# The low half of every second weight chunk of six output panels, made by an adding DMA instead of VectorE

## The chip, the cores and the metric

The program runs on one NeuronCore of one Trainium2 chip, in one launch. The metric is the device time of one execution in microseconds (us), taken as the median of three executions. Beside it stands one profiled execution, from which every duration below comes.

## The reference

The layer takes 256 tokens of width 4096 and 256 memory tokens. One input projection makes the columns of three head groups and their gates, the groups are computed, gated and concatenated, and one output projection with a residual and a layer norm ends it. Everything is float32.

```
proj = x @ w_in                      # (256 x 4096) @ (4096 x 11280)
c_a, c_b, c_gate, g_q, g_k, g_v, g_lr, g_gate, m_q, m_gate = split(proj)
y_conv = conv_group(c_a, c_b, ...) * silu(c_gate)
y_gla  = gla_group(g_q, g_k, g_v, g_lr, ...) * silu(g_gate)
y_mem  = memory_group(m_q, mem @ w_mem_kv) * silu(m_gate)
mixed  = concatenate([y_conv, y_gla, y_mem])
out    = mixed @ w_out               # (256 x 4096) @ (4096 x 4096)
x      = layernorm(2**0.25 * x + out) * ln_g + ln_b
```

## The kernel before

[...] ScalarE rounds `raw` to `hi` (line 89) and VectorE subtracts to get `lo` = `raw` - `hi` (line 90). A product is then three passes: hi by hi, hi by the activation's low half, and lo by hi.

All weight matrices are cut into panels of up to 512 columns, and a panel into 16 chunks of two blocks of 128 rows each. A chunk is a tile of 128 partitions by 1024 float32, 512 KB. The function `panel` runs over the chunks of one panel: it loads a chunk from memory on SyncE's DMA queue (line 115), splits it, and issues 12 matmuls (line 279), for two token tiles of 128: eight that read `hi` and, behind them, four that read `lo`. The work comes in this order: memory keys and values (lines 146 to 180), 23 panels of the input projection with the three head groups' own work woven in, and 8 panels of the output projection (lines 934 to 952, here n = 0 to 7).

The tiles that carry the chunks come from pools: six buffers for `raw`, four for `hi` and four for `lo`. So ScalarE can round a chunk only when TensorE is done with the `hi` of four chunks before, and a load can start only when an earlier `raw` has been read for the last time. Every engine works through its own queue in order. The order within the queues is made by a scheduler when the program is built, and semaphores tie the queues together.

At the end of an output panel VectorE adds the panel's two banks to the residual (line 929) and takes its statistics (line 932), and GpSimd multiplies the panel by a row of the norm's gain (line 946), which a small DMA has spread over the partitions (line 924). The last panel, n = 7, holds its last six chunks in other buffers and ends one token tile before the other, so that the final norm can overlap.

Of the kernel before, what the change touches and what calls it, by code (L numbers as in the profile page):

```python
# [9 lines left out]
F32 = mybir.dt.float32  # L10
F32R = mybir.dt.float32r
BF16 = mybir.dt.bfloat16
AF = mybir.ActivationFunctionType
ALU = mybir.AluOpType
# [3 lines left out]
P = 128  # L18
D = 4096
KT = D // P  # L20
# [9 lines left out]

C_A, C_B, C_G, G_Q, G_K, G_V, G_LR, G_G, M_Q, M_G = 0, 1024, 2048, 3072, 4096, 5120, 7168, 7184, 9232, 10256

# (name, index, column ranges of w_in)
PANELS = (
    [("cb", 0, [(C_B, 512)]), ("ca", 0, [(C_A, 512)])]
    + [("cb", 1, [(C_B + 512, 512)]), ("ca", 1, [(C_A + 512, 512)])]
# [12 lines left out]
def layer_kernel(ctx, tc, xT, memT, xres, w_mem, w_in, w_out, cst, w_gate,  # L49
                 conv_g, conv_b, norm_g, ln_g, ln_b, out):  # L50
    nc = tc.nc
# [8 lines left out]
    acc = ctx.enter_context(tc.tile_pool(name="acc", bufs=4, space=PSUM))  # L60
    sm = ctx.enter_context(tc.tile_pool(name="sm", bufs=4, space=PSUM))

    # SBUF in units of 4 KB a partition, each handed out again once it is given back
    free_units = deque(range(NUNITS))
    unit_of = {}
    serial = [0]
# [18 lines left out]
        return small.tile([P, n], F32, tag=f"little{n}", name=f"{name}_{serial[0]}")  # L85

    def halves(src, hi, lo):
        """fp32 as hi + lo, each exact in the 12 bits the PE multiplies."""
        nc.scalar.copy(out=hi, in_=src)  # L89
        nc.vector.tensor_tensor(out=lo, in0=src, in1=hi.bitcast(F32), op=ALU.subtract)  # L90

# [17 lines left out]
            unit([P, 4, 256], F32R, f"l{name}"),  # L109
        )  # L110

    def load(tiles, ap, a=None, b=None):
        """DRAM -> raw -> hi + lo, of columns or k-tiles a to b."""
        raw, hi, lo = (t[:, a:b] for t in tiles)
        nc.sync.dma_start(out=raw, in_=ap[:, a:b])  # L115
        halves(raw, hi, lo)
        return tiles[1], tiles[2]

    work = deque()
    fill = deque()  # L120

    def do_work(n):
        """Up to n pieces of queued work; None ends the turn."""
        for _ in range(min(n, len(work))):
            f = work.popleft()
            if f is None:
                break
            f()
# [1 line left out]
    def pause(n=1):  # L130
        work.extend([None] * n)

# [1 line left out]
    def four(ap):  # L134
        return ap.rearrange("p (k t) -> p k t", k=4)

# [2 lines left out]
    mem_banks = [acc.tile([P, 512], F32, tag="acc", name=f"mk_{i}") for i in range(4)] + [  # L139
        bank("mv") for _ in range(4)  # L140
    ]
    # the array's clock comes up while the first loads are under way
    idle = nc.const_aps.tensor(1.0, [P, 512], BF16)
    for _ in range(WARM):
        nc.tensor.matmul(mem_banks[7], lhsT=idle[:, 0:P], rhs=idle, start=True, stop=True)
# [53 lines left out]
        for mt in range(2):  # L199
            halves(mem_banks[4 + nb * 2 + mt], mvh[nb][:, mt, :], mvl[nb][:, mt, :])  # L200

    # A transpose without the PE: DVE transposes the 32 x 32 blocks in their places, copies between
    # groups of 32 partitions put the blocks where they belong
    def queue_transpose(src, dst, then, back=False):
        """Token-major [P, 2, 512] -> feature-major [P, 4, 256], or back. dst() is asked for the
        tile when the first block moves; then(tile) is queued behind the last."""
        st = {}

        def blocks():
            t = tmp.tile([P, 1024], F32, tag="T", name=f"T_{serial[0]}", bufs=1)  # L210
            serial[0] += 1
            nc.vector.transpose(out=t, in_=src.rearrange("p a b -> p (a b)"))  # L212
            give(src)
            st["t"] = t

        def moves(b):
            if b == 0:
                st["d"] = dst()
            tok = "p t (q j c) -> p t q j c"
            feat = "p q (t i c) -> p t q i c"  # L220
            flat = "p (q t i c) -> p t q i c" if back else "p (t q j c) -> p t q j c"
            sizes = dict(q=4, t=2, c=32)
            frm = st["t"].rearrange(flat, **sizes)
            to = st["d"].rearrange(tok if back else feat, c=32, **({"q": 4} if back else {"t": 2}))
            for a in range(4):
                f = nc.scalar.copy if a % 2 else nc.vector.tensor_copy
                f(  # L227
                    out=to[32 * b : 32 * b + 32, :, :, a, :],
                    in_=frm[32 * a : 32 * a + 32, :, :, b, :],
                )  # L230

        work.append(blocks)
        for b in range(4):
            work.append(lambda b=b: moves(b))
        work.append(lambda: then(st["d"]))

    def queue_halves(src, then):
        """Token-major [P, 2, 512] -> feature-major hi and lo, for then(hi, lo)."""

        def scratch():  # L240
            serial[0] += 1
            return tmp.tile([P, 4, 256], F32, tag="S", name=f"S_{serial[0]}", bufs=1)

        def go(d):
            hi, lo = unit([P, 4, 256], F32R, "xh"), unit([P, 4, 256], F32R, "xl")
            halves(d, hi, lo)
            then(hi, lo)

        queue_transpose(src, scratch, go)
# [3 lines left out]
        queue_halves(mk[i], lambda hi, lo, i=i: mkT.update({i: (hi, lo)}))  # L253

    def products(ps, terms):
        """Sum over (stationary hi, lo), (moving hi, lo) pairs of three exact passes each."""
        n = len(terms)
        for t, ((sh, sl), (mh, ml)) in enumerate(terms):
            for k, (a, b) in enumerate(((sh, mh), (sl, mh), (sh, ml))):
                nc.tensor.matmul(  # L260
                    ps, lhsT=a, rhs=b, start=t == 0 and k == 0, stop=t == n - 1 and k == 2
                )

# [1 line left out]
    def panel(chunks, width, stat, fills=0, apart=0, soon=KT // 2):  # L265
        """stat(kt // 4) gives the stationary hi and lo. The products of the last `apart` chunks
        are left to the caller, as a function of the chunk's place and the token tile."""
        banks = []
        for tt in range(2):
            serial[0] += 1  # L270
# [15 lines left out]

        for c in range(KT // 2):
            tiles = w_tiles([P, 2, width], "w", KT // 2 - apart <= c < KT // 2 - WBUFS)
            hi, lo = load(tiles, chunks[c].rearrange("p (k n) -> p k n", k=2))
            if c >= KT // 2 - apart:  # L290
                held.append((c, hi, lo))
            else:
                for w in (hi, lo):
                    for tt in range(2):
                        mms(c, tt, w, w is lo)
            left = max(1, soon - c)
            do_work(-(-len(work) // left))
            for _ in range(min(fills, len(fill))):
                fill.popleft()()
# [10 lines left out]
    mixT = {}  # L310

    def queue_mix(src, key):
        """Token-major mixed columns -> feature-major hi and lo."""
        queue_halves(src, lambda hi, lo: mixT.update({key: (hi, lo)}))

# [1 line left out]
    mo = {}  # L317

    def queue_memory(i, mq):
# [73 lines left out]
        pause(2)  # L393
        work.append(probs)

# [1 line left out]
    qT, kT, v, o = {}, {}, {}, {}  # L397
    gate = {}

    def queue_lr(lr):  # L400
        def weights():
            # rows 0-15 and 32-47 hi, rows 64-79 lo, against hi, lo and hi of lr
            raw = unit([P, 1024], F32, "wgraw")
            w = unit([P, 1024], F32R, "wg")
            nc.gpsimd.memset(raw, 0.0)
            for r in (0, 32, 64):
                nc.sync.dma_start(out=raw[r : r + 16, :], in_=w_gate)
            nc.scalar.copy(out=w, in_=raw)
            nc.vector.tensor_tensor(
                out=w[64:96, :], in0=raw[64:96, :], in1=w[64:96, :].bitcast(F32), op=ALU.subtract  # L410
            )
            give(raw)
            gate["w"] = w
# [16 lines left out]
        pause(2)  # L430

    def queue_gates(i):
        """Decays of heads 2*i, 2*i+1, applied to queries and keys."""
        st = {}

        def logits(pair):
# [71 lines left out]
            give(kT[i])  # L508

        def composites():  # L510
            # ca: [end-decayed 0 | 1] for chunk 1, [end-decayed 0, through chunk 1 | end-decayed 1]
            # for chunks 2 and 3; cb: [end-decayed 2 | 3] for chunk 3, queries [2 | 3 through chunk 2]
            kt_, ks, el, q = gate[i][0], st["cs"], st["el"], qT[i]
            ca = unit([P, 4, 256], F32, "ca")
            cb = unit([P, 4, 256], F32, "cb")
# [27 lines left out]
    def queue_head(h):  # L543
# [3 lines left out]
        def attn():  # L547
# [21 lines left out]
            for nm in ("Ah", "Al"):  # L569
                st["a"].append(tmp.tile([P, 512], F32R, tag=nm, name=f"{nm}_{h}", bufs=1))  # L570
            halves(ps[:, :384], *(t[:, :384] for t in st["a"]))
            # keys s of a tile against tokens c of the same tile: keep c >= s
            for t in st["a"]:
                diag = t.rearrange("p (t c) -> p t c", t=2)[:, :, 0:P]
                nc.gpsimd.affine_select(
# [41 lines left out]
        work.append(lambda: outputs(0))  # L617
        work.append(lambda: outputs(1))

# [1 line left out]
    conv = {"h": {}, "y": {}}  # L621

    def queue_conv(i):
# [85 lines left out]
            for tt in range(2):  # L709
                work.append(lambda i=i, tt=tt: norm(i, tt))  # L710

# [1 line left out]
    sig = {}  # L713
    off = 0
    for name, i, ranges in PANELS:
# [93 lines left out]
        give(hi, lo)  # L809
    assert not fill  # L810

# [1 line left out]
    keys = [("gla", i) for i in range(4)] + [("conv", i) for i in range(2)] + [  # L813
        ("mem", i) for i in range(2)
    ]

    # y = (z g) rstd - mu rstd g + b: z g as z comes, the rest a product of -mu rstd and 1
    # with g and b, g hi in rows 0 and 32, lo in 64, b hi in row 1, lo in 65
    gb = []

    def rows_gb(j):
# [16 lines left out]
    def stat(u):  # L838
        return mixT[keys[u]]

    z = []
# [92 lines left out]
    for n in range(8):  # L934
# [3 lines left out]
        nc.sync.dma_start(out=xr, in_=xres[n].rearrange("p (t d) -> p t d", t=2))  # L938
        z.append(xr)
        if n < 7:  # L940
            banks = panel(w_out[n], 512, stat, soon=KT // 2 if n else 10)
            g = spread(ln_g, n, "S")
            for tt in range(2):
                residual(tt, n, banks[tt])
                y = z[n][:, tt, :]
                nc.gpsimd.tensor_tensor(out=y, in0=y, in1=g, op=ALU.mult)

    # the last panel ends with the first token tile, so that its norm runs beside the second's
    banks, rest = panel(w_out[7], 512, stat, apart=APART)
    g, beta = spread(ln_g, 7, "S"), spread(ln_b, 7, "Ah")  # L950
    for k in range(APART):
# [104 lines left out]
```

## Time and profile before

| what | value |
|---|---|
| three executions | 1541.36, 1542.34, 1542.21 us; median 1542.21 us |
| profiled execution, first to last instruction | 1539.6 us |
| difference between that span and the median | 2.6 us (1542.21 - 1539.6) |
| TensorE's granted clock, mean of the span | 0.997 |
| ScalarE and GpSimd, busy | 740.7 us (48%) and 68.0 us (4%) |
| moved by DMA | 307.56 MB, mean 200 GB/s |
| all DMA issues | on SyncE's queue; none on GpSimd's |

The time of the profiled execution is known by its span alone, from its first to its last instruction; the 2.6 us around it are launch and end, as far as the two numbers can be compared. The share of busy time of an engine is an average over the whole span. What a stage is worth is read from that stage: which engine has no gap there, and which wait ends last. The busy time of matmuls overlaps, since each starts before the one ahead has left the array, so their rate is read from a chain of many.

### The profile page before, as it was taken

What the parts mean: (1) busy time and instruction counts of PE and PEld (TensorE: products, weight loads), DVE (VectorE), ACT (ScalarE), POOL (GpSimd) and SP (SyncE); (2) the same over time, 40 slices, a digit from 0 to 9 for tenths busy, and PEclk for the clock granted to TensorE, in tenths of its full rate; (3) what the DMA queues carried; (4) which work ended last, traced back from release to release, by engine and by line L of the source; (5) the groups of instructions that cost most, each with busy time, mean ns of one, the idle gap of its engine ahead of it and who ended that gap; (6) DMA issues with size and microseconds to landing.
All of it is one profiled execution on the core that took longest, in us unless ns stands there. A gap on an engine that the chain in (4) does not pass through costs nothing.

```text
span 1539.6 us, 18667 instructions
## 1 busy us (share of the span) xinstructions
PE 1526.9 (99%) x6977; PEld 1292.9 (84%) x6977; DVE 980.6 (64%) x1227; ACT 740.7 (48%) x898; POOL 68.0 (4%) x71
## 2 busy tenths in 40 slices
PE   9999999999999999999999999999999999999997
PEld 7888888888888888999998888888888888888885
DVE  6555654999999555857575555555557555455555
ACT  6444653444566344655454554455556333333341
POOL 0000000000000000003030000000000000000001
PEclk9999999999999999999999999999999999999998
DMA  8777676666656666565555566666677666666662
GB/s 326 245 251 249 190 210 193 190 197 188 193 163 178 218 192 188 161 191 175 167 170 195 179 195 205 193 193 195 195 233 253 216 196 196 206 202 199 198 199 109
DMA packets 89363, 307.56 MB, mean 200 GB/s; under 512 B 9972, under 2 KB 10868, under 8 KB 89272
## 3 DMA queue, kind: packets, MB, share of 16 engines
q1 hardware_dynamic: 89272, 306.38, 63.0%
q8 instruction: 54, 0.88, 0.2%
q14 instruction: 37, 0.30, 0.1%
HBM read 302.14 MB, written 4.19 MB: 199 GB/s over the span
## 4 chain that ended last, share of the span: by engine, by line
PE 98%; DVE 1%; DMA 0%; issue 0%; SPq 0%; ACT 0%; POOL 0%; DVEq 0%; ACTq 0%
PE acc L279 85%; PE mk L169 5%; PE mv L169 5%; PE o L260 1%; PE A L561 1%; PE sc L260 0%; PE mo L260 0%; DMA rawwm<-w_mem 0%; DVE xr L915 0%; SPq L115 0%; PE mg L905 0%; DVE nz L502 0%; POOL xr L913 0%; DVE cc L870 0%; DVE low L90 0%
## 5 line engine op out<-in xcount | busy, mean ns | idle before, releaser
L90 DVE TENSOR_TENSOR low<-raww,hiw 128x1024 fp32r<-128x1024 f32 (+2 forms) x496 | 603.5, 1219 | 427.5 <-ACT hiw L89 422.3
L89 ACT CAST hiw<-raww 128x1024 fp32r<-128x1024 f32 (+2 forms) x496 | 507.6, 1027 | 640.7 <-PE acc L279 612.4
L279 PE MATMUL acc<-hiw,hx 128*128 128x512 f32 (+2 forms) x1472 | 560.3, 381 | 0.0
L279 PE MATMUL acc<-hiw,lx 128*128 128x512 f32 (+2 forms) x1472 | 560.3, 381 | 0.0
L279 PE MATMUL acc<-low,hx 128*128 128x512 f32 (+2 forms) x1472 | 381.6, 380 | 0.0
L279 PEld LDWEIGHTS acc<-hiw,hx 128*128 128x128 f32 x1472 | 276.4, 188 | 45.4
L279 PEld LDWEIGHTS acc<-hiw,lx 128*128 128x128 f32 x1472 | 276.3, 188 | 45.2
L279 PEld LDWEIGHTS acc<-low,hx 128*128 128x128 f32 x1472 | 275.3, 188 | 45.4
L279 PE MATMUL acc<-hiw,xh 128*128 128x512 f32 x512 | 199.3, 389 | 0.0
L279 PE MATMUL acc<-hiw,xl 128*128 128x512 f32 x512 | 199.2, 389 | 0.0
L279 PE MATMUL acc<-low,xh 128*128 128x512 f32 x512 | 137.8, 389 | 0.0
L279 PEld LDWEIGHTS acc<-hiw,xl 128*128 128x128 f32 x512 | 96.1, 188 | 20.0
L279 PEld LDWEIGHTS acc<-low,xh 128*128 128x128 f32 x512 | 96.1, 188 | 19.9
L279 PEld LDWEIGHTS acc<-hiw,xh 128*128 128x128 f32 x512 | 96.1, 188 | 19.9
L90 DVE TENSOR_TENSOR lowm<-rawwm,hiwm 128x1024 fp32r<-128x1024 f32 (+2 forms) x68 | 78.3, 1160 | 53.2 <-ACT hiwm L89 52.6
L649 DVE SCALAR_TENSOR_TENSOR cacc<-hT,cst_sb,cacc 128x231 f32<-128x231 f32 (+29 forms) x240 | 98.0, 462 | 0.1
L89 ACT CAST hiwm<-rawwm 128x1024 fp32r<-128x1024 f32 (+2 forms) x68 | 67.6, 1002 | 62.8 <-PE mv L169 30.9
L169 PE MATMUL mk<-hiwm,hmem 128*128 128x512 f32 (+1 forms) x132 | 50.7, 387 | 0.4 <-ACT hiwm L89 0.4
L169 PE MATMUL mk<-hiwm,lmem 128*128 128x512 f32 (+1 forms) x132 | 50.4, 384 | 0.0
L227 ACT COPY S<-T 32x256 f32<-32x256 f32 x112 | 45.2, 404 | 9.9 <-DVE T L212 8.5
L169 PE MATMUL mv<-hiwm,hmem 128*128 128x512 f32 x128 | 49.9, 390 | 0.0
L169 PE MATMUL mv<-hiwm,lmem 128*128 128x512 f32 x128 | 49.8, 389 | 0.0
(179 smaller groups left out, 752.5 us busy)
## 6 DMA issues: line engine op xcount, KB each, us to landing
raww<-w_in SPq DMA_DIRECT2D x288, 512.0 KB
raww<-w_out SPq DMA_DIRECT2D x128, 512.0 KB
rawwm<-w_mem SPq DMA_DIRECT2D x62, 512.0 KB
raww<-w_in SPq DMA_DIRECT2D x64, 412.0 KB
raww<-w_in SPq DMA_DIRECT2D x16, 416.0 KB
rawx<-xT SPq DMA_DIRECT2D x8, 512.0 KB
xr<-xres SPq DMA_DIRECT2D x8, 512.0 KB
out<-xr SPq DMA_DIRECT2D x16, 256.0 KB
```

Of the source, the lines that this page charges most:

```text
L89: nc.scalar.copy(out=hi, in_=src)
L90: nc.vector.tensor_tensor(out=lo, in0=src, in1=hi.bitcast(F32), op=ALU.subtract)
L169: nc.tensor.matmul(mem_banks[half * 4 + a // 512 * 2 + mt][:, a % 512 : a % 512 + step], lhsT=s[:, kt % 4, mt * P : (mt + 1) * P], rhs=w[: ...
L227: f(out=to[32 * b : 32 * b + 32, :, :, a, :], in_=frm[32 * a : 32 * a + 32, :, :, b, :],)
L260: nc.tensor.matmul(ps, lhsT=a, rhs=b, start=t == 0 and k == 0, stop=t == n - 1 and k == 2)
L279: nc.tensor.matmul(banks[tt][:, :width], lhsT=s[:, kt % 4, tt * P : (tt + 1) * P], rhs=w[:, k, :], start=kt == 0 and not second and s is s ...
L561: nc.tensor.matmul(ps[:, at : at + n], lhsT=keys[:, j, k0 : k0 + P], rhs=qs[:, j, q0 : q0 + n], start=dk == 0, stop=dk == 1,)
L649: nc.vector.scalar_tensor_tensor(out=a, in0=h, scalar=dw_sb[:, cb, j : j + 1], in1=a, op0=ALU.mult, op1=ALU.add)
```

## The change

In the output panels n = 1 to 6 the chunks with an odd number (8 of 16 in each panel, 48 in all) get their low half in another way. ScalarE rounds `raw` to `hi` as before, then writes -`hi` into `lo`. A DMA issued from GpSimd's queue then reads `raw` and adds it to `lo` in place, in SBUF. The subtraction on VectorE is left out for these chunks. Even chunks, the other panels and the rest of the program keep the subtraction. The diff, without the comments and text that it also takes out:

```diff
-    def load(tiles, ap, a=None, b=None):
+    def load(tiles, ap, a=None, b=None, added=False):
         raw, hi, lo = (t[:, a:b] for t in tiles)
         nc.sync.dma_start(out=raw, in_=ap[:, a:b])
-        halves(raw, hi, lo)
+        if added:
+            nc.scalar.copy(out=hi, in_=raw)
+            nc.scalar.activation(out=lo, in_=hi.bitcast(F32), func=AF.Copy, scale=-1.0)
+            nc.gpsimd.dma_start(out=lo.bitcast(F32), in_=raw, accum_op=ALU.add)
+        else:
+            halves(raw, hi, lo)
         return tiles[1], tiles[2]
...
-    def panel(chunks, width, stat, fills=0, apart=0, soon=KT // 2):
+    def panel(chunks, width, stat, fills=0, apart=0, soon=KT // 2, added=False):
...
-            hi, lo = load(tiles, chunks[c].rearrange("p (k n) -> p k n", k=2))
+            hi, lo = load(tiles, chunks[c].rearrange("p (k n) -> p k n", k=2), added=added and c % 2 == 1)
...
-            banks = panel(w_out[n], 512, stat, soon=KT // 2 if n else 10)
+            banks = panel(w_out[n], 512, stat, soon=KT // 2 if n else 10, added=n > 0)
```

The order of TensorE's queue does not change: 5935 instructions in the same places. ScalarE's queue gains 48 instructions, each right behind the rounding of its chunk; VectorE's loses 48.

GpSimd's queue around the end of panel 0, before. `gbraw` is a buffer for the last norm, and `xr` the residual that is multiplied by the gain row, once per panel:

```order
L825 MEMSET gbraw_10896 128x1024
L946 TENSOR_TENSOR xr_9320<-xr_9320,row_9636 128x512 x2
L946 TENSOR_TENSOR xr_9644<-xr_9644,row_9936 128x512 x2
L946 TENSOR_TENSOR xr_9944<-xr_9944,row_10246 128x512 x2
L946 TENSOR_TENSOR xr_10254<-xr_10254,row_10556 128x512 x2
```

The same place now (lines are six higher from here on). The first two DMAs are those of chunks 1 and 3 of panel 1, the next six those of its chunks 5 to 15, and the two behind them chunks 1 and 3 of panel 2:

```order
L831 MEMSET gbraw_10928 128x1024
L120 DMA low_9668<-raww_9666 128x1024
L120 DMA low_9705<-raww_9703 128x1024
L952 TENSOR_TENSOR xr_9320<-xr_9320,row_9636 128x512 x2
L120 DMA low_9742<-raww_9740 128x1024
L120 DMA low_9779<-raww_9777 128x1024
L120 DMA low_9816<-raww_9814 128x1024
L120 DMA low_9853<-raww_9851 128x1024
L120 DMA low_9890<-raww_9888 128x1024
L120 DMA low_9927<-raww_9925 128x1024
L120 DMA low_9986<-raww_9984 128x1024
L120 DMA low_10023<-raww_10021 128x1024
```

Eight DMAs per panel have come between the multiplications, two of them ahead of the multiplication that ends the panel before.

SyncE's queue in the first half of panel 1, before, with the queues that each load waits for. The loads are those of chunks 6 to 10 (`raww_733` to `raww_737`); `DVE` is VectorE, and `DMAHW` an earlier DMA of SyncE:

```order
L115 DMA raww_733_9756<-w_out 128x1024 [waits DMAHW3_49,DVE_49]
L115 DMA raww_734_9774<-w_out 128x1024 [waits DMAHW4_49,DVE_49]
L115 DMA raww_735_9792<-w_out 128x1024 [waits DMAHW5_49,DVE_49]
L115 DMA raww_736_9810<-w_out 128x1024 [waits DMAHW6_49,DVE_49]
L115 DMA raww_737_9828<-w_out 128x1024 [waits DMAHW7_49,DVE_49]
```

And now, where `DMASW0` and `DMASW1` are the adding DMAs of chunks 1 and 3:

```order
L116 DMA raww_733_9759<-w_out 128x1024 [waits DMAHW3_49,DVE_49]
L116 DMA raww_734_9777<-w_out 128x1024 [waits DMAHW5_49,DVE_49]
L116 DMA raww_735_9796<-w_out 128x1024 [waits DMAHW4_49,DMASW0_49]
L116 DMA raww_736_9814<-w_out 128x1024 [waits DMAHW7_49,DVE_49]
L116 DMA raww_737_9833<-w_out 128x1024 [waits DMAHW6_49,DMASW1_49]
```

The loads stand in the same order, but every second one now waits for an adding DMA to end: chunk 8 takes the buffer of chunk 1, chunk 7 that of chunk 2.

## Rows read from the trace of the kernel before

**Rows 1.** Page, part 1: busy time and share of each engine.

```profile
PE 1526.9 (99%) x6977; PEld 1292.9 (84%) x6977; DVE 980.6 (64%) x1227; ACT 740.7 (48%) x898; POOL 68.0 (4%) x71
```

**Rows 2.** Page, part 4: the chain that ended last, share by engine.

```profile
PE 98%; DVE 1%; DMA 0%; issue 0%; SPq 0%; ACT 0%; POOL 0%; DVEq 0%; ACTq 0%
```

**Rows 3.** Chain of waits from 1180 us to 1300 us: start, length, what.

```profile
1179.79 120.36 PE acc L279 x531
```

**Rows 4.** Windows: stretch, length, busy (count) by engine, clock, DMA share, GB/s.

```profile
core 0: us, PE busy (x) PEld busy (x) DVE busy (x) ACT busy (x) POOL busy (x), PEclk, DMA share, GB/s
10.00:16.00 6.00, 5.60 (x25) 4.30 (x24) 4.38 (x5) 4.54 (x5) 0.00 (x0) 1.00 1.03 408
1214.00:1470.00 256.00, 256.00 (x1132) 212.03 (x1131) 136.16 (x119) 99.18 (x94) 21.20 (x12) 1.00 0.63 199
```

**Rows 5.** Groups by line, 1177 us to 1480 us: count, busy, mean ns, idle before.

```profile
L90 DVE TENSOR_TENSOR low<-raww,hiw 128x1024 fp32r<-128x1024 f32 x111 | 142.6, 1286 | 133.1 <-ACT hiw L89 133.0
L89 ACT CAST hiw<-raww 128x1024 fp32r<-128x1024 f32 x112 | 118.2, 1055 | 179.4 <-PE acc L279 172.7 <-DVE low L90 6.7
```

**Rows 6.** Timeline of ScalarE, final norm: an activation that scales.

```profile
1518.01 1.34 ACT L911 ACTIVATE xr<-xr,zrs 128x512 f32<-128x512 f32 x2 [11.18 <-POOL zrs L859]
```

**Rows 7.** Timeline, panel 1, ScalarE, TensorE, VectorE, SyncE: start, length, what, idle before.

```profile
1238.83 0.33 SPq L115 DMA_DIRECT2D raww<-w_out  x1
1239.01 0.62 PE L279 MATMUL acc<-low,xh 128*128 128x512 f32 x2
1239.21 1.05 ACT L89 CAST hiw<-raww 128x1024 fp32r<-128x1024 f32 x1 [1.67 <-PE acc L279]
...
1240.30 1.23 DVE L90 TENSOR_TENSOR low<-raww,hiw 128x1024 fp32r<-128x1024 f32 x1 [1.50 <-ACT hiw L89]
...
1249.89 0.62 PE L279 MATMUL acc<-low,xh 128*128 128x512 f32 x2
```

**Rows 8.** Timelines of SyncE and ScalarE, panel 7: two loads that ScalarE waited for.

```profile
1484.59 0.33 SPq L115 DMA_DIRECT2D raww<-w_out  x1
...
1486.83 2.57 SPq L115 DMA_DIRECT2D raww<-w_out  x2
...
1487.96 1.05 ACT L89 CAST hiw<-raww 128x1024 fp32r<-128x1024 f32 x1 [0.17 <-DMA raww<-w_out]
1491.36 2.95 ACT L89 CAST hiw<-raww 128x1024 fp32r<-128x1024 f32 x3 [2.35 <-DMA raww<-w_out]
```

**Rows 9.** Timeline of GpSimd: its smallest operation, in the final norm.

```profile
1516.99 0.98 POOL L859 TENSOR_TENSOR zrs<-zrs,negh 128x1 f32<-128x1 f32 x1 [31.27 <-DVE zmn L862]
```

**Rows 10.** Timelines around the end of panel 0: VectorE, GpSimd, ScalarE.

```profile
1217.90 1.28 DVE L929 SCALAR_TENSOR_TENSOR xr<-xr,acc 128x512 f32<-128x512 f32 x2 [0.86 <-PE acc L279]
...
1221.01 3.53 POOL L946 TENSOR_TENSOR xr<-xr,row 128x512 f32<-128x512 f32 x2 [45.19 <-DVE zstats L932]
...
1221.44 1.94 DVE L90 TENSOR_TENSOR low<-raww,hiw 128x1024 fp32r<-128x1024 f32 x1
...
1222.89 1.05 ACT L89 CAST hiw<-raww 128x1024 fp32r<-128x1024 f32 x1 [1.66 <-PE acc L279]
```

**Rows 11.** Waits of SyncE's queue, 1190 us to 1480 us: total, times, longest.

```profile
SPq L115 <- DVE low L90: 238.5, 107, 2.9
SPq L924 <- POOL xr L946: 4.9, 6, 0.8
```

**Rows 12.** Line 946, all 14 of its instructions: least, median and longest ns.

```profile
L946 POOL TENSOR_TENSOR xr<-xr,row x14: 1291/1791/2293, 1221.0 to 1483.4; 128x512 f32<-128x512 f32 x14
```

## The prediction, made before the changed kernel ran

> **What bounds the kernel now.** I first read part 1 of the page [rows 1]: TensorE is busy for 1526.9 of 1539.6 us, so all its gaps together are 12.7 us, while VectorE is at 64% and GpSimd at 4%. Then the chain that ended last [rows 2]: 98% of it is TensorE. An average over stages could still hide a gap where the change is, so next came the chain in that place [rows 3]: from 1179.79 us it is one unbroken piece of 531 matmuls in 120.36 us, 226.7 ns each. A chunk of 12 matmuls takes 2.72 us, and the 96 chunks of the six panels 261.1 us. The window over the panels says the same: 256.00 us busy of 256.00 us [rows 4]. There TensorE waits for nobody, and no work taken from another engine can shorten it. VectorE waits there itself (133 us for ScalarE), and ScalarE waits for TensorE (172.7 us) [rows 5]: the three follow TensorE. So the question is only whether the new way of making `lo` is ready in time, every time.
>
> **What goes.** 48 subtractions of 1.286 us [rows 5], 61.7 us of VectorE. They lie beside matmuls and VectorE has gaps, so this is worth 0.
>
> **What ScalarE gains.** 48 negations of a 128x1024 tile. The rounding of the same tile costs 1.055 us [rows 5]; a scaling activation took 1.34 us for two tiles of half that width [rows 6]. So 1.06 to 1.34 us each; I take 1.06, the row of the same tile. ScalarE's turn for a chunk is 2.72 us with a gap of 1.67 us behind the rounding [rows 7], and the negation fits there. The `lo` buffer it writes is free by then: the matmuls on the old `lo` take 4 x 0.227 = 0.91 us, the rounding beside them 1.055 us. Cost 0.
>
> **How long the adding DMA may take.** ScalarE starts to round a chunk at 1239.21 us, when TensorE has just left the `hi` of four chunks before; the four matmuls on that older chunk's `lo` start at 1239.01 us, and those on the new chunk's `lo` at 1249.89 us [rows 7], 10.88 us or four chunks on. Rounding and negation end at 1239.21 + 1.055 + 1.06 = 1241.32 us. From there to 1249.89 us are 8.57 us (8.3 with the dearer negation). As long as a DMA from GpSimd, issue to landing, takes less, TensorE sees nothing. Over it, a ring sets the pace: four matmuls on `lo` (0.91 us), negation (1.06 us), DMA (A), and again, every four chunks. Its period is 1.97 + A against 10.88 us, with 24 such periods in six panels, so past A = 8.91 us each further us costs 24 us.
>
> **How long it takes.** The trace has no adding DMA and none from GpSimd, so I bound it. Two loads of the same 512 KB that ScalarE had to wait for were issued at 1484.59 and 1486.83 us and used at 1487.96 and 1491.36 us: 3.37 and 4.53 us [rows 8]. The lower bound is the first, 3.37 us. For the upper I add to the second: one more pass over 512 KB for the second operand at the fastest rate that the trace shows, 408 GB/s [rows 4], 1.285 us; as much again for a load whose packets interleave; and 0.98 us for GpSimd's smallest operation [rows 9], as an estimate of the issue. That is 8.08 us. Without the interleaved load it is 6.8 us, my value: the row of 4.53 us already ran among other loads. All three are under 8.57 us, the upper one by 0.5 us only.
>
> **What the DMA engines can carry.** In the six panels they move 199 GB/s at a share of 0.63, and at the start of the program 408 GB/s at a share of 1.03 [rows 4]; I take 408 for full. An adding DMA every second chunk is 524,288 bytes per 5.44 us, 96.4 GB/s for each time that its bytes pass. One pass would make 199 + 96 = 295 GB/s (72% of 408), two passes (two reads beside one write) 392 (96%), three, each read and write paid, 488 (120%). The transfer reads two tiles and writes one, so two passes is the row's natural reading, and it fits with little to spare. One and three are the bounds.
>
> The Trainium skill has a rule for this price (Collectives: The Full Stack, "The bandwidth ceiling: the fold count and why AG ≠ RS ≠ AR"): a reducing transfer is slower than a copy by its two source reads and not by the addition, measured as 1.93 to one. By that, an estimate, the load is 199 + 1.93 x 96.4 = 385 GB/s, and it fits too; no row here shows a reducing transfer.
>
> **What moves in the queues.** GpSimd's queue is in order, with two adding DMAs ahead of each panel-end multiplication. That multiplication ran from 1221.01 to 1224.54 us, and ScalarE starts to round the next added chunk, number 5, at 1222.89 us [rows 10]; its DMA is ready to go at 1222.89 + 2.12 = 1225.01 us, 0.5 us after. Before that, chunk 3's DMA is ready near 1219.6 us, ahead of the multiplication. So neither waits for the other; if the multiplication came 2 us late, the DMA of chunk 5 would be late by 1.5 us, six times, within the slack of 1.8 us that A = 6.8 leaves. The gain row's small DMA on SyncE waits for that multiplication (4.9 us in six times [rows 11]), with loads behind it, and keeps its place.
>
> `raw` is held longer. Before, its load's successor goes out when the subtraction ends, 2.32 us after the rounding began (1240.30 + 1.23 - 1239.21) [rows 7]; VectorE is what SyncE waits for [rows 11]. Now chunk 8 takes the buffer of chunk 1 and goes out 2.12 + 6.8 = 8.9 us after chunk 1's rounding, lands 4.53 us later, at 13.4 us, and is rounded at 7 x 2.72 = 19.0 us. The loads behind it on SyncE are held up too, but the next is not due for release before 8.16 + 2.32 = 10.5 us. Cost 0, up to A = 12.4 us.
>
> **The sum.** 0 + 0 + 0 on the profiled execution's 1539.6 us span, so the median of the runs shown stays: **1542.2 us** (2.6 us lie around the span). What the DMAs hide behind is the four-deep `hi` and `lo` buffers.
>
> **Rivals.**
>
> *The DMA engines are full* (slower). From more than (408 - 199) / 96.4 = 2.17 passes on, loads and additions need more time than the panels have, and TensorE waits for its weights. At three passes, 488 / 408 = 1.196, the 261.1 us grow by 51 us: 1593 us. For it: the margin at two passes is 4%, and the 408 GB/s come from loads out of memory alone. Against it: share and rate at the full stretch agree, and 199 GB/s at 0.63 extrapolates to 316 GB/s only because packets at low load also count their waiting.
>
> *The adding DMA lands late* (slower). If it reads back, adds and writes as two landings in a row, A = 2 x 4.53 + 1.285 + 0.98 = 11.3 us, the ring takes 13.3 us for four chunks, 24 x 2.4 = 57 us more: 1600 us. A milder form is GpSimd being held up while it issues. The multiplications of line 946 took 1291 to 2293 ns [rows 12] with VectorE's subtractions beside them, one of these stretched to 1.94 us [rows 10]: the two engines do get in each other's way. One subtraction of 1.23 us on top of the upper 8.08 us makes A = 9.3 and 24 x 0.4 = 9.6 us: 1552 us. Against it: all my bounds from single landings are under 8.57 us.
>
> The Trainium skill (SBUF — State Buffer, "Who interferes with whom") says that GpSimd, which writes the descriptors for its DMAs, is shut out of a shared port while VectorE runs in a two-port mode, and that a two-input operation takes only the read side. By the first, DMAs would stall beside copies; by the second the subtractions hold back only GpSimd work that reads, like line 946, which the trace bears out.
>
> *Faster.* VectorE's relief would have to speed the matmuls or the end. For it only that line 946 may drop from its median of 1.79 to its least of 1.29 us. Against it: no gap of TensorE in the six panels, and panel 7 with the final norm keeps its order. A gain over 0.2% would need 3.1 us of the 12.7 us of gaps, which lie outside these panels: 1539 us.
>
> **Chances and range.** No change 0.55; engines full 0.25; late landing 0.16; faster 0.04. So slower 0.41. Changes under 0.2% (3.1 us) I count as none, since a measurement of this kernel can hardly tell them. The likeliest case's own range is 1541.0 to 1545. The whole range goes up to the three-pass case, 1593 us, and leaves out the late landing in its full form and still dearer passes, some 0.15, and below 1541.0 us about 0.04.
>
> **What the profile after would show.** Right: TensorE busy through the whole window of the six panels, DMA from GpSimd landing within 8.5 us, ScalarE's turn still 2.72 us, no wait of TensorE for an adding DMA. The moved GB/s and share tell the passes. Wrong by full engines: a DMA share near 1 in that window, and ScalarE waiting for loads of `raw`. Wrong by late landing: a share well under 1, and matmuls on `lo` waiting for adding DMAs every second chunk. The forecast falls if one addition needs over 2.17 passes or 8.6 us.

## The result and the profile after

The changed kernel takes 1551.21 us (median of 3 runs, 1548.93 to 1551.46) against 1542.21 us before. The ratio is 1.0055, with a 95% interval of 1.0036 to 1.0075, so it is slower by 9 us, where no change was forecast. A second measurement of the same kernel, beside new runs of the kernel before, gave 1550.37 us against 1541.93, ratio 1.0056 (1.0044 to 1.0068). The profiled execution took 1551.46 us with a span of 1549.7 us; the numbers below are from it. Six lines were added ahead of the panel code, so the matmuls of line 279 now stand at 285. Line 116 loads, 118 rounds an added chunk, 119 negates it, 120 issues the adding DMA, and 952 is the multiplication that was 946.

First the page: its span, part 1 (busy time), the queue of the adding DMAs from part 3 (packets, MB, share of the DMA engines), the chain from part 4, and the negation from part 5.

```profile
span 1549.7 us, 18771 instructions
PE 1529.5 (99%) x6977; PEld 1292.4 (83%) x6977; DVE 927.5 (60%) x1179; ACT 791.5 (51%) x946; POOL 104.2 (7%) x119
...
q0 software_dynamic: 6912, 25.17, 8.5%
...
PE 87%; DMA 9%; issue 2%; DVE 1%; POOL 0%; ACT 0%; SPq 0%; DVEq 0%; POOLq 0%; ACTq 0%
...
L119 ACT ACTIVATE low<-hiw 128x1024 fp32r<-128x1024 f32 x48 | 50.9, 1060 | 9.1 <-PE acc L285 7.8
```

TensorE's busy time grew by 2.6 us only [rows 1], the span by 10.1: the rest are gaps. DMA, which had 0% of the chain [rows 2], now has 9%. That is not 9% of lost time: the chain runs from one DMA to the next, and TensorE works beside most of it. The negation cost 1060 ns.

The window over the six panels (stretch, length, busy by engine, clock, DMA share, GB/s) shows where the gaps are:

```profile
1214.00:1470.00 256.00, 249.60 (x1093) 204.01 (x1091) 81.69 (x69) 144.47 (x137) 55.64 (x58) 1.00 1.00 281
```

TensorE was busy for all of the 256 us [rows 4] and now misses 6.4. The DMA engines went from a share of 0.63 to 1.00. Their 281 GB/s count each added byte once, so the rate alone doesn't show that they are full; the share does.

The waits between 1177 and 1490 us (who waits for what, total us, times, longest):

```profile
PEld acc L285 <- DMA low<-raww: 9.8, 9, 2.0
ACT low L119 <- PE acc L285: 7.8, 7, 1.8
PE acc L285 <- DMA low<-raww: 6.4, 7, 1.6
```

TensorE waits for the adding DMA 7 times. ScalarE's 7 waits in front of the negation follow from these. No row has ScalarE waiting for `raw`.

The instructions of line 120 (ns least, median, longest) and the time from issue to landing of the 48 transfers:

```profile
L120 POOL DMA_DIRECT2D low<-raww x48: 862/869/1042, 1215.2 to 1479.7; - x48
...
DMA to landing us min/median/max: 4.9/7.0/10.1
```

The median of 7.0 us is under the slack of 8.57 us that the prediction worked out; the longest is not. One of the late transfers, in the timelines of ScalarE, GpSimd, SyncE and TensorE (start, length, what, idle before):

```profile
1316.34 1.06 ACT L119 ACTIVATE low<-hiw 128x1024 fp32r<-128x1024 f32 x1
...
1317.70 0.88 POOL L120 DMA_DIRECT2D low<-raww  x1 [2.01 <-ACT low L119]
...
1318.01 0.33 SPq L116 DMA_DIRECT2D raww<-w_out  x1
1318.39 0.42 SPq L930 DMA_DIRECT2D row<-ln_g  x1
1320.32 10.76 SPq L116 DMA_DIRECT2D raww<-w_out  x4
...
1326.77 1.20 PE L285 MATMUL acc<-low,xh 128*128 128x512 f32 x4 [0.67 <-DMA low<-raww]
```

And the chain of waits where this transfer ends (start, length, what):

```profile
1312.26 14.47 DMA low<-raww x2
1326.73 0.04 issue
1326.77 87.43 PE acc L285 x384
```

The negation ends at 1317.40, GpSimd issues 0.30 us later (0.29 to 0.32 us in all 48), and the DMA lands at 1326.73, 9.33 us after the negation. Less the slack of 8.57 that is 0.76 us, and TensorE's row says that it sat idle for 0.67. Around the issue stand two weight loads, issued at 1316.82 and 1318.01, and the gain row.

The same subtraction can be made for every transfer from the trace's issue and landing times. 8 of the 48 land more than 8.57 us after their negation (8.62 to 10.38), by 7.5 us in all. From the first matmul of panel 1 to the first of panel 7 TensorE takes 269.89 us, by the matmul starts of the trace, where it took 261.12 before: 8.8 us (8.4 if only the steps with a visible wait are summed, the number that an expectation below uses). So most of the 10.1 us by which this profiled span is longer are these few late landings.

### The profile page after: what moved, and what is told of

It reads as the page before. It is cut to its first block, busy times and chain, and to the rows that moved or that the text cites. A ratio compares the mean times of both kernels' runs of the same rounds, so it can differ in the third digit from the quotient of the medians.

```text
span 1549.7 us, 18771 instructions
## 1 busy us (share of the span) xinstructions
PE 1529.5 (99%) x6977; PEld 1292.4 (83%) x6977; DVE 927.5 (60%) x1179; ACT 791.5 (51%) x946; POOL 104.2 (7%) x119
## 4 chain that ended last, share of the span: by engine, by line
PE 87%; DMA 9%; issue 2%; DVE 1%; POOL 0%; ACT 0%; SPq 0%; DVEq 0%; POOLq 0%; ACTq 0%
PE acc L285 74%; DMA low<-raww 8%; PE mk L175 5%; PE mv L175 5%; PE o L266 1%; PE A L567 1%; DMA rawwm<-w_mem 0%; PE sc L266 0%; PE mo L266 0%; DVE xr L921 0%; SPq L116 0%; POOL xr L952 0%; ACT low L119 0%; ACT hiw L118 0%; POOL low L120 0%
## 5 line engine op out<-in xcount | busy, mean ns | idle before, releaser
L90 DVE TENSOR_TENSOR low<-raww,hiw 128x1024 fp32r<-128x1024 f32 (+2 forms) x448 | 549.7, 1230 | 492.2 <-ACT hiw L89 487.1
L89 ACT CAST hiw<-raww 128x1024 fp32r<-128x1024 f32 (+2 forms) x448 | 457.0, 1024 | 512.5 <-PE acc L285 490.8
L118 ACT CAST hiw<-raww 128x1024 fp32r<-128x1024 f32 x48 | 50.6, 1054 | 79.9 <-PE acc L285 79.9
L120 POOL DMA_DIRECT2D low<-raww x48 | 41.9, 874 | 246.6 <-ACT low L119 146.9
L119 ACT ACTIVATE low<-hiw 128x1024 fp32r<-128x1024 f32 x48 | 50.9, 1060 | 9.1 <-PE acc L285 7.8
```

What stands on the lines that cost most here:

```text
L118: nc.scalar.copy(out=hi, in_=raw)
L119: nc.scalar.activation(out=lo, in_=hi.bitcast(F32), func=AF.Copy, scale=-1.0)
L120: nc.gpsimd.dma_start(out=lo.bitcast(F32), in_=raw, accum_op=ALU.add)
```

## The experiments

All times are medians, with the kernel before run on the same chip at 1541.8 to 1542.0 us. Each edit is made to the changed kernel, and each window is that of 1214 to 1470 us, with its columns as above.

**The addition by VectorE, everything else as changed.**

```diff
-            nc.gpsimd.dma_start(out=lo.bitcast(F32), in_=raw, accum_op=ALU.add)
+            nc.vector.tensor_tensor(out=lo, in0=raw, in1=lo.bitcast(F32), op=ALU.add)
```

> The 48 chunks keep ScalarE's negation, but VectorE adds raw to it where the change has the DMA from GpSimd. Theory (the DMA engines are nearly full, so the adding DMA's time scatters from 4.9 to 10.1 us around 7.0, and the 8 of 48 that run over the slack of 8.57 us cost about 1 us each): the loss goes entirely, 1542.2 us within 0.2%, no wait of TensorE in the six panels. Rival (ScalarE's extra 48 x 1.06 us delays the rounding): part of the 9 us stays, 1545 us or more.

Measured: 1542.07 us, ratio 1.0001 (0.9991 to 1.0011).

```profile
1214.00:1470.00 256.00, 256.00 (x1131) 211.99 (x1130) 140.02 (x118) 149.37 (x142) 21.20 (x12) 1.00 0.64 199
```

ScalarE does its 48 negations (149 us busy), TensorE has no gap. The negations are free; the loss is in the DMA.

**The same DMAs without the addition.** `lo` then holds `raw`.

```diff
-            nc.gpsimd.dma_start(out=lo.bitcast(F32), in_=raw, accum_op=ALU.add)
+            nc.gpsimd.dma_start(out=lo.bitcast(F32), in_=raw)
```

> The DMA from GpSimd copies raw over lo instead of adding to it, so the low halves of these chunks are not those of the reference. Same issue, same bytes written, one operand read less. Theory: packets of 4 KB at about 159 ns instead of 328, landing in 4 to 6.5 us, DMA share about 0.85, no wait of TensorE, 1542 us. Rival (GpSimd's software-issued path makes the DMA late, whatever it reads): landings and stalls as with the addition, 1549 to 1551 us.

Measured: 1542.72 us, ratio 1.0005 (0.9996 to 1.0014). The window over the panels:

```profile
1214.00:1470.00 256.00, 256.00 (x1131) 211.99 (x1130) 82.15 (x71) 149.32 (x143) 41.31 (x59) 1.00 0.86 293
```

The issues of line 120, and their landings:

```profile
L120 POOL DMA_DIRECT2D low<-raww x48: 540/540/755, 1215.7 to 1471.3; - x48
...
DMA to landing us min/median/max: 3.2/5.2/7.1
```

The queue of these DMAs, from part 3 of the page:

```profile
q0 software_dynamic: 6912, 25.17, 4.3%
```

As many DMAs, bytes and issues, and no loss. The addition doubles what the transfers take of the engines, 8.5% against 4.3%; single 4 KB packets took 328 and 159 ns in the median. No 4 KB packet of an adding DMA took under 327 ns, in the next run either, where the share is 0.84, so the longer packets are not an effect of full engines. So the loss comes with the addition; its second read and its arithmetic are not told apart by any run here.

**Every fourth chunk, 24 adding DMAs.**

```diff
-            hi, lo = load(..., added=added and c % 2 == 1)
+            hi, lo = load(..., added=added and c % 4 == 1)
```

> Only chunks 1, 5, 9 and 13 of the six panels get the adding DMA (24 instead of 48). Theory: the DMA engines are at a share of about 0.82, no landing over 8.5 us, 1542 to 1543 us. Rival (GpSimd's path, a fixed price for each): half of the loss, 1546 to 1547 us.

Measured: 1542.19 us, ratio 1.0001 (0.9992 to 1.0011).

```profile
1214.00:1470.00 256.00, 256.00 (x1131) 211.99 (x1130) 104.17 (x95) 124.74 (x119) 42.31 (x36) 1.00 0.84 246
```

The landings:

```profile
DMA to landing us min/median/max: 4.7/4.8/6.2
```

At a share of 0.84 an adding DMA of 512 KB lands in 4.8 us in the median and 6.2 at the longest.

**Every chunk, 96 adding DMAs.**

```diff
-            hi, lo = load(..., added=added and c % 2 == 1)
+            hi, lo = load(..., added=added)
```

> All 16 chunks of the six panels get the adding DMA (96 instead of 48). This shows what one addition costs the DMA engines when they are the bound. Two passes each (a packet of 328 ns beside a load's 159): a chunk needs 8 x (159 + 328) = 3.90 us of an engine instead of TensorE's 2.72, 96 x 1.18 = 113 us more, 1655 us. Three passes: about 1780 us. If the loss were a fixed 1 us for every sixth DMA by another cause: about 1560 us.

Measured: 1644.06 us, one run. The window:

```profile
1214.00:1470.00 256.00, 208.14 (x813) 153.70 (x812) 12.41 (x20) 141.67 (x135) 71.99 (x78) 0.97 1.05 274
```

The main waits between 1177 and 1490 us:

```profile
ACT hiw L118 <- DMA raww<-w_out: 118.2, 66, 5.4
PEld acc L285 <- DMA low<-raww: 74.9, 58, 3.1
```

Two of ScalarE's rounds, from its timeline:

```profile
1400.93 1.05 ACT L118 CAST hiw<-raww 128x1024 fp32r<-128x1024 f32 x1 [1.72 <-DMA raww<-w_out]
...
1404.68 1.04 ACT L118 CAST hiw<-raww 128x1024 fp32r<-128x1024 f32 x1 [1.61 <-DMA raww<-w_out]
```

This is what full engines look like: now ScalarE waits for weights too. A chunk takes 1404.68 - 1400.93 = 3.75 us. One load and two passes of the addition, 3 x 512 KB, are then 419 GB/s, against 408 in [rows 4]; with three passes they would be 559. So it is two passes, and a capacity near 410. The 1655 us that were expected by two passes come near the 1644.06.

**A fifth pair of `hi` and `lo`.** In a quarter of the chunks the pair is taken from scratch memory. The other chunks then find their pair free earlier, and an adding DMA can start earlier before its `lo` is needed.

```diff
+            if added and c % 4 == 0:
...
+                hi = tmp.tile([P, 1024], F32R, tag="T", name=f"hiw_{m}", bufs=1)
...
+                lo = [tmp.tile([P, 512], F32R, tag=g, name=f"low{g}_{m}", bufs=1) for g in ("Al", "fifth")]
...
```

> The change, with a fifth pair of hi and lo buffers in the six panels: every fourth chunk (one with a subtraction) uses it, so that the added chunks find their buffers free at least one chunk, 2.72 us, earlier. The adding DMAs are the same 48. Theory (the DMA engines carry the load on average, 96% by two passes, and only the scatter of the landings over the slack of 8.57 us costs): the slack is 11.3 us or more against a latest landing of 10.4 us after the negation, so no wait of TensorE is left, 1542 to 1543 us, with the DMA share still about 1. Rival (the engines are over-full on average): deeper buffers only put the waits off, 1547 us or more.

Measured: 1546.33 us (1543.16 to 1549.49, 8 runs), ratio 1.0027 (1.0016 to 1.0037): about half of the loss is gone, less than the theory said and more than the rival.

```profile
1214.00:1470.00 256.00, 254.28 (x1114) 208.66 (x1113) 84.69 (x91) 140.28 (x137) 55.01 (x58) 1.00 1.02 282
```

The landings of line 120:

```profile
DMA to landing us min/median/max: 4.9/7.4/10.5
```

The waits between 1177 and 1490 us:

```profile
ACT hiw L118 <- DMA raww<-w_out: 95.1, 37, 4.9
...
PE acc L285 <- DMA low<-raww: 1.7, 2, 1.0
```

The landings are as scattered as in the change, but TensorE's 7 waits for them became 2. What came instead is ScalarE waiting for `raw`, 95 us where the change has none: with more room at one end, the engines that are full show at the other. Before it rounded each of the two chunks that TensorE still waited for, ScalarE had itself waited 2.8 us for `raw`. Not all that is left is the DMA's: panels without a wait take 43.79 us here against 43.52 before, by the matmul starts, which is 1.6 us in six panels and comes with this edit. More `raw` buffers weren't tried, since no memory is left for them.

**The gain row.** Its DMA waits on SyncE for the multiplication of the panel before, with loads behind it. Two buffers for it in one kernel, and in another only panel 0's row loaded, which leaves the right gain out of panels 1 to 6; a third kernel is the change again.

```diff
-            g = spread(ln_g, n, "S")
+            g = spread(ln_g, n, "ST"[n % 2])
```

```diff
-            g = spread(ln_g, n, "S")
+            if n == 0:
+                g = spread(ln_g, n, "S")
```

> The change, with the gain rows in two buffers by turns, so that SyncE's row DMA behind a panel's end no longer waits for GpSimd's multiplication of that panel. 7 of the 8 late landings were within the first nine chunks of a panel. If that wait holds the weight loads back and bunches them: most of these go, 1543 to 1546 us. If the bunching comes from the buffers that the adding DMAs hold: no difference from the change, 1548 to 1552 us.

> The change, with the gain row of panel 0 used for panels 1 to 6 too (the norm's gain is wrong there): six row DMAs of 256 KB and their waits are left out. The same two readings as for the two buffers, and in addition the rows' own bytes: if either sets the late landings, 1543 to 1546 us; if not, 1548 to 1552 us.

> The change itself once more, on the same chip as the three others, with more runs: 1548 to 1552 us by every theory; its landings again scatter around 7 us, with 6 to 12 of 48 over 8.57 us after the negation.

Measured: 1548.25 us (ratio 1.0049, 1.0037 to 1.0061), 1550.25 us (1.0053, 1.0041 to 1.0065) and, for the change again, 1550.37 us (1.0056, 1.0044 to 1.0068). The intervals overlap: no effect of the row that could be told. A part of 1 or 2 us isn't excluded.

**Half of each added chunk, 48 DMAs of 256 KB.** VectorE subtracts the other half.

```diff
...
-            nc.gpsimd.dma_start(out=lo.bitcast(F32), in_=raw, accum_op=ALU.add)
...
+            nc.gpsimd.dma_start(out=lo[:, 0].bitcast(F32), in_=raw[:, 0], accum_op=ALU.add)
+            nc.vector.tensor_tensor(out=lo[:, 1], in0=raw[:, 1], in1=hi[:, 1].bitcast(F32), op=ALU.subtract)
```

> All 48 chunks keep their adding DMA, but for the first of their two blocks only (256 KB); VectorE subtracts the second. As many DMAs from GpSimd as in the change, half the bytes. Theory (engine time and the scatter of landings near full load): share about 0.82 to 0.85, landings of 3 to 6 us, no wait of TensorE, 1542 to 1543 us. Rival (a price per DMA): the loss stays, 1548 to 1551 us.

Measured: 1542.25 us, ratio 1.0004 (0.9995 to 1.0013).

```profile
1214.00:1470.00 256.00, 256.00 (x1131) 212.02 (x1131) 107.04 (x119) 129.27 (x142) 62.21 (x59) 1.00 0.86 244
```

The landings:

```profile
DMA to landing us min/median/max: 3.4/5.5/7.9
```

As many adding DMAs as in the change, with half the bytes: none lands over 8.57 us after its negation, and nothing is lost.

**Fewer loads beside unchanged adding DMAs.** Of the chunks that aren't added only the first half is loaded, and used for both.

```diff
+            if added and c % 2 == 0:
...
+                nc.sync.dma_start(out=raw[:, 0], in_=src[:, 0])
+                for k in range(2):
+                    halves(raw[:, 0], hi[:, k], lo[:, k])
...
```

> All 48 adding DMAs stay as in the change, 512 KB each, but of the other 48 chunks of the six panels only the first half (256 KB) is loaded and used twice, so half of those weights is left out. The loads fall from 199 to 199 - 48 x 262,144 bytes / 261.1 us = 151 GB/s; with two passes of 96.4 GB/s for the additions that is 344 of 408 GB/s, 84% instead of 96%. Theory (the late landings come from DMA engines that are nearly full): the share is about 0.85 to 0.9, no landing takes over 8.6 us, the median is near 5 to 5.5 us, TensorE is busy through the whole window, 1542 to 1543 us. Rival (an adding DMA of 512 KB every second chunk lands late by itself, whatever the loads do): landings still 7 us in the median and up to 10, 1548 to 1551 us.

Measured: 1542.94 us, ratio 1.0007 (0.9998 to 1.0016).

```profile
1214.00:1470.00 256.00, 255.62 (x1127) 211.17 (x1127) 88.14 (x118) 152.64 (x189) 56.52 (x59) 1.00 0.95 245
```

Line 120: who waited for it (us, times), and the landings:

```profile
  PE acc L285: 0.4, 1
...
DMA to landing us min/median/max: 4.9/6.0/8.7
```

The time came as the theory said, with the same 48 transfers of 512 KB: what else the engines carry makes them late. The sizes were missed: share 0.95 where 0.85 to 0.9 was expected, and median 6.0 where 5 to 5.5 was. The longest landing was 8.7 us, with one wait of TensorE of 0.4 us, where no landing over 8.6 us and no wait were expected.

**Two of three chunks, 60 adding DMAs, and the same with lighter loads.**

```diff
-            hi, lo = load(..., added=added and c % 2 == 1)
+            hi, lo = load(..., added=added and c % 3 > 0)
```

> Two of three chunks of the six panels get the adding DMA (60 instead of 48). If the engines' time decides: 96 loads of 8 x 0.159 us and 60 additions of 8 x 0.328 us are 279.5 us of each engine, or 272.5 us at the rate of the run with all 96 (3.80 us a chunk instead of 3.90), against 261.1 us of matmuls: 11 to 18 us over, and the scatter on top, 1556 to 1568 us. If each adding DMA had a fixed mean price (8.4 us / 48): 60 x 0.175 = 10.5 us, 1552 us.

> Two of three chunks are added, 60 adding DMAs, which cost 42 us before; but of the 36 other chunks only the first half is loaded and used twice, so half of those weights is left out. Loads 199 - 36 x 262,144 bytes / 261.1 us = 163 GB/s, additions 2 x 120.5 = 241, together 404 of 408 GB/s, 99% instead of 108%. Theory (the loss is the DMA engines' time, and grows steeply only past 100%): 1545 to 1560 us. Rival (the uneven order, two adding DMAs in a row and then none, with the waits that it puts into the queues, makes most of the 42 us): still above 1570 us.

Measured: 1583.74 us, ratio 1.0272 (1.0253 to 1.029), and 1565.69 us, ratio 1.0156 (1.0142 to 1.017). Both are dearer than the theory said, and the second lies below the rival. Line 120 with whole loads, who waited for it (us, times) and the landings:

```profile
  PE acc L285: 27.9, 29
...
DMA to landing us min/median/max: 4.7/8.9/12.3
```

The same with the lighter loads, below their window over the panels:

```profile
1214.00:1470.00 256.00, 245.80 (x1053) 195.09 (x1051) 55.77 (x88) 153.57 (x176) 63.25 (x68) 1.00 1.00 257
...
  PE acc L285: 13.3, 21
...
DMA to landing us min/median/max: 4.7/8.2/11.3
```

The step that failed in these expectations is the same as in the prediction: the time was worked out from the mean load of the engines. Counted by landings it agrees better:

| kernel | landings over 8.57 us | their excess, us | TensorE late in the six panels, us |
|---|---|---|---|
| copies; every fourth; halves | 0 | 0 | 0 |
| lighter loads | 2 of 48 | 0.6 | 0.8 |
| gain row of panel 0 only | 6 of 48 | 4.4 | 5.6 |
| the change | 8 of 48 | 7.5 | 8.8 |
| the change again | 10 of 48 | 6.7 | 7.8 |
| gain rows in two buffers | 9 of 48 | 7.4 | 8.3 |
| two thirds, lighter loads | 28 of 60 | 29.7 | 24.2 |
| two thirds | 42 of 60 | 54.8 | 42.7 |

The columns are from the negation, issue and landing times and the matmul starts of each trace, so each row is that of one profiled execution. The kernel with one gain row was profiled in one of its shorter executions, 1547.51 us of 1547.28 to 1553.24. In the last two rows TensorE loses less than the excess; that a chunk which comes late also puts off when the next is needed would explain it, but was only argued. Why two thirds with lighter loads, at 99% by count, land at 8.2 us in the median and the change, at 96%, at 7.0 stays open; the share is 1.00 in both windows and doesn't tell them apart. That two adding DMAs there follow each other 2.7 us apart was argued, not isolated.

## Why the prediction was wrong

**What bounds the kernel, what goes, ScalarE.** Right. VectorE's 61.7 us were worth nothing, the negation cost 1.06 us and stays free when VectorE adds (1542.07 us).

**How long the adding DMA may take.** Right to 0.3 us: 8.57 us after the negation is the line past which TensorE waits, as the transfer at 1317.70 and the table show. The prediction set it against issue to landing and left out the 0.30 us before the issue, so a transfer really had 8.27 us.

**How long it takes, and the sum.** This step failed: the sum put 0 for the wait on the adding DMAs, and 8.8 us were measured. The value of 6.8 us was nearly the median (7.0), in part by luck, since the same transfer took 4.8 us at a share of 0.84. But the sum used it for all 48 transfers, and the upper bound of 8.08 us was passed by 10 of them: the longest took 10.1. The bound had room for one load whose packets interleave, while the trace has two loads and the gain row around one late issue. Fewer loads took all but two of the late landings away, and other gain rows didn't; which packets held up this one transfer is not shown. A margin of 1.8 us on the mean isn't one on the slowest sixth. A late landing costs its own excess, about 1 us, and eight of them came; the ring of the prediction, which sets the pace when every landing is late, did not form.

**What the DMA engines can carry.** The two passes were right (8.5% against 4.3%), and so was "fits with little to spare" for the mean. The error was to read 96% as no cost. Between a share of 0.84 and one of 1.00 the median landing of the same 512 KB went from 4.8 to 7.0 us and its longest from 6.2 to 10.1. The rule of the Trainium skill that was weighed there (Collectives: The Full Stack, "The bandwidth ceiling: the fold count and why AG ≠ RS ≠ AR"), two source reads against one, 1.93, agrees with the packets here, 328 / 159 = 2.06.

**The queues.** Right: the issue came 0.30 us after the negation, the multiplications were not in the way, and `raw` was no limit in the change (no wait of ScalarE for it).

**The rivals.** It was neither as priced. The engines did not need more time than the panels have, as in the first, nor did all landings come late, as in the second; but the second's condition, a landing later than its slack, was met 8 times because the first's margin was too thin. The 1552 us of the milder late landing is close only by chance: it put a stall of GpSimd behind it, and the issues show none.

## What to carry to other kernels

Hold a transfer's slack against the slowest of its landings, not against the mean, as soon as the DMA engines' share nears 1: here 0.84 to 0.86 cost nothing, 0.95 nothing clear of noise, and 1.00 cost 9 us, with the mean still inside the slack. Count an adding DMA as two passes of its bytes, and read the share, since the GB/s show one; but a share of 1.00 stood beside losses of 9 and of 24 us, so past that count the late landings. Another buffer for the result moved the wait in part to the loads, with the engines full; fewer bytes took it away.

## What the runs showed of the hardware that was not expected

- The row of an adding DMA's issue is 0.87 us long at the median, that of the plain copy of the same tile 0.54 (line 120 above). But the issue doesn't hold GpSimd for so long: the multiplication behind it starts 0.57 us after the issue does, and 0.57 to 0.58 us in all six panels (0.56 behind the copy):

```profile
1312.26 0.86 POOL L120 DMA_DIRECT2D low<-raww  x1 [4.58 <-ACT low L119]
1312.83 2.86 POOL L952 TENSOR_TENSOR xr<-xr,row 128x512 f32<-128x512 f32 x2
```

- The subtraction of VectorE beside GpSimd's multiplication, one in each of the six panels, took 3.15 to 3.19 us in the change, against a mean of 1.286 in [rows 5] and 1.94 in the same place before [rows 10]:

```profile
1222.02 3.19 DVE L90 TENSOR_TENSOR low<-raww,hiw 128x1024 fp32r<-128x1024 f32 x1 [0.87 <-ACT hiw L89]
```
